# Second FFN block of a transformer layer: where the late tokens' pieces are loaded from, and on which queue

## The chip, the cores and the metric

One Trainium2 chip, one of its cores. The metric is device time in microseconds (us) of the whole kernel, one launch; a lower number is better. Five engines run side by side, each through its own instruction queue: TensorE (PE in the profile; PEld are its weight loads), VectorE (DVE), ScalarE (ACT), GpSimd (POOL) and SyncE (SP). SP, ACT and POOL can also issue DMA transfers. "SPq" and "POOLq" in a row mean the issue of a DMA on that queue.

## The reference

One layer for 128 context tokens and 1024 latent tokens of width 1024, all in float32:

```python
x <- LN(alpha*x + 0.5 * gate1 * SwiGLU_1(mod1(x)))     # first FFN block
x <- LN(alpha*x + gate2 * Mixer(mod2(x)))              # attention, pooling, gates
x <- LN(alpha*x + 0.5 * gate3 * SwiGLU_2(mod3(x)))     # second FFN block

def _modulate(x, shift, scale):
    return x * (1.0 + scale) + shift

def _swiglu(h, w1, w2):                                # w1: 1024 x 5632, w2: 2816 x 1024
    a, b = jnp.split(h @ w1, 2, axis=-1)
    return (jax.nn.silu(a) * b) @ w2
```

Only the second FFN block (`SwiGLU_2`) and the way its input comes out of the mixer matter here.

## The kernel before

Every float32 product is three matmuls: `split` (L107 on ACT, L108 on DVE) makes a high and a low part of each operand, and `mm3` (L130 to L132) adds high-high, high-low and low-high. The FFN products are arranged as Strassen-like sums: seven products of half blocks in place of eight, so both operands also have to be added and subtracted before they are split.

The latent tokens form two halves of 512: half n = 0 is tokens 0 to 511 of the latent rows, half n = 1 the late tokens. For each half and each of the 8 blocks of 128 channels (`kc`) there is one *piece*, a 128 x 512 tile. `piece_dram(n, kc)` makes one: it loads a token-major block from `x2_d[1 + n]` (the mixer's result, in DRAM), transposes it on PE in four 128 x 128 steps (L135) into a PSUM bank, and modulates it on ACT (L402) into its final place. One such load is 256 KB in 512 runs of 512 bytes.

`x2_d` is written by `norm_tile` as the mixer's last token tiles are normalized (L350, a DMA on POOL's queue, tile names `x<-ry`). The last group of three token tiles holds the end of the late half, so half n = 1 is complete only when the last of those stores has landed. These last normalizations run inside `lead_first`, beside the products `A11` of the first four feature blocks.

Then `lead` runs with `begun` true. In program order it does: `second` (product `A12`) for p = 0 to 3; `first_sum` (weights minus weights, L711) for four p, two loads each; four pieces of half 0 into `self.first`; then for k = 0 to 3 `sum_operands` (L457), which takes pieces (1, k) and (1, k+4), adds them and splits the sum into `S1[k]` (tile `b`), each followed by the units of product `S1` for p = 0 and 1; product `S1` for p = 2; the other four pieces of half 0; product `S1` for p = 3; `next_operand` (`S2`, L462); and then the products `S2`, `S4`, `S3`, `A22` with their weights (L738, L752, L756) and `last_operands` (L468, L471).

Two sets of places matter. `raw_tile` is a ring of 5 places of 4 KB per partition through which nearly all raw loads go, weights and pieces alike, all issued on SP's queue in order; a load waits there until the place it takes is free. The tag `b2` has 12 places of 4 KB per partition: in this block eight of them first hold the pieces of half 0 (tile `xp`), and later all are used for the left operands `S3`, `S4` and `A22`. The pieces of half 1 end in tile `pc`. Instructions are put into each engine's queue at build time by a scheduler which takes, in program order, those that it thinks are ready; so the order within a queue can differ from the order in the code, and is fixed before the kernel runs.

Of the kernel before, what the change touches and what calls it, by code (L numbers as in the profile page):

```python
# [25 lines left out]
F32 = mybir.dt.float32  # L26
# [6 lines left out]
P = 128  # L33
# [21 lines left out]
class Layer:  # L55
# [362 lines left out]
        return m  # L418

    def piece_dram(self, n, kc):  # L420
        r = self.raw(self.x2_d[1 + n][:, :, kc * P : (kc + 1) * P], 512)
        b = self.bank()
        for t in range(4):
            self.transpose(b[:, t * P : (t + 1) * P], r[:, t * P : (t + 1) * P])
        m = self.piece_place(n, kc)
        self.modulated(m, b, 2, LAT, kc)
        return m
# [1256 lines left out]
```

## Time and profile before

| | |
|---|---|
| median of 3 runs | 2496.45 us (2493.36 to 2497.18) |
| the profiled execution | 2495.49 us, its span 2493.7 us |
| granted TensorE clock, mean | 0.995 |
| PE busy | 2452.3 us (98% of the span) |
| DVE busy | 1830.6 us (73%) |
| ACT busy | 1214.5 us (49%) |
| POOL busy | 463.4 us (19%) |
| DMA, SP's queue | 373.79 MB, 44.7% of 16 engines' span |
| DMA, POOL's queue | 86.32 MB, 9.3% of 16 engines' span |

PE is busy nearly all of the span, so the time is read from where PE is idle and from what ends each of its idle stretches. "Released by" means the event that came last before the waiting instruction began. Share figures are averages over the span; a change in one stage is read from that stage alone.

### The profile page before, as it was taken

What the parts mean: (1) busy time and instruction counts of PE and PEld (TensorE: products, weight loads), DVE (VectorE), ACT (ScalarE), POOL (GpSimd) and SP (SyncE); (2) the same over time, 40 slices, a digit from 0 to 9 for tenths busy, and PEclk for the clock granted to TensorE, in tenths of its full rate; (3) what the DMA queues carried; (4) which work ended last, traced back from release to release, by engine and by line L of the source; (5) the groups of instructions that cost most, each with busy time, mean ns of one, the idle gap of its engine ahead of it and who ended that gap; (6) DMA issues with size and microseconds to landing.
All of it is one profiled execution on the core that took longest, in us unless ns stands there. A gap on an engine that the chain in (4) does not pass through costs nothing.

```text
span 2493.7 us, 34226 instructions
## 1 busy us (share of the span) xinstructions
PE 2452.3 (98%) x12297; PEld 2115.0 (85%) x12297; DVE 1830.6 (73%) x2817; ACT 1214.5 (49%) x2094; POOL 463.4 (19%) x691
## 2 busy tenths in 40 slices
PE   8999999999999999999999999999899999999998
PEld 4788888888889989889999999998688888887887
DVE  6877778877678556566888886876877666676877
ACT  5544444444445343434778773435744344444442
POOL 0000011110022212232567640110000001111002
PEclk9999999999999999999999999999999999999999
DMA  7455566778686555534100035665754445558773
GB/s 292 144 167 188 182 224 230 244 259 326 213 276 218 184 180 189 188 136 163 42 1 2 1 110 187 237 215 185 223 173 164 150 173 195 205 197 320 269 267 121
DMA packets 167554, 463.75 MB, mean 186 GB/s; under 512 B 18900, under 2 KB 37636, under 8 KB 167384
## 3 DMA queue, kind: packets, MB, share of 16 engines
q1 hardware_dynamic: 140952, 373.79, 44.7%
q0 software_dynamic: 23696, 86.32, 9.3%
q8 instruction: 97, 1.59, 0.3%
q10 hardware_dynamic: 2736, 1.44, 0.2%
q14 instruction: 73, 0.60, 0.1%
HBM read 390.42 MB, written 71.07 MB: 185 GB/s over the span
## 4 chain that ended last, share of the span: by engine, by line
PE 84%; DVE 6%; issue 4%; DMA 3%; ACT 2%; POOL 1%; SPq 0%; DVEq 0%; POOLq 0%; ACTq 0%
PE w L130 24%; PE w L131 24%; PE w L132 24%; PE w L1060 8%; PE w L135 3%; DVE op L108 1%; DVE x L108 1%; DMA raw<-w 1%; DVE mx L1389 1%; PE w L224 0%; DMA yc<-fc 0%; ACT pr L1397 0%; DMA raw<-w1c 0%; DVE so L108 0%; DMA raw<-x 0%
## 5 line engine op out<-in xcount | busy, mean ns | idle before, releaser
L107 ACT ACTIVATE op<-raw 128x1024 fp32r<-128x1024 f32 (+1 forms) x505 | 483.9, 969 | 517.4 <-PE w L131 263.4
L108 DVE TENSOR_TENSOR op<-raw,op 128x1024 fp32r<-128x1024 f32 (+1 forms) x505 | 558.9, 1116 | 233.1 <-ACT op L107 201.1
L130 PE MATMUL w<-b,op 128*128 128x512 f32 x880 | 343.9, 393 | 7.1 <-ACT b L107 2.9
L131 PE MATMUL w<-b,op 128*128 128x512 f32 x880 | 344.6, 392 | 0.0
L132 PE MATMUL w<-b,op 128*128 128x512 f32 x880 | 339.7, 391 | 0.3 <-DVE op L108 0.3
L130 PE MATMUL w<-x,op 128*128 128x384 f32 x768 | 260.0, 339 | 0.0
L131 PE MATMUL w<-x,op 128*128 128x384 f32 x768 | 258.8, 337 | 0.0
L132 PE MATMUL w<-x,op 128*128 128x384 f32 x768 | 257.7, 337 | 0.0
L131 PE MATMUL w<-op,so 128*128 128x512 f32 (+1 forms) x627 | 242.4, 387 | 2.0 <-DVE op L108 2.0
L132 PE MATMUL w<-op,so 128*128 128x512 f32 (+1 forms) x627 | 241.9, 387 | 0.0
L130 PE MATMUL w<-op,so 128*128 128x512 f32 (+1 forms) x627 | 232.7, 386 | 1.0 <-ACT op L107 0.9
L130 PEld LDWEIGHTS w<-b,op 128*128 128x128 f32 x880 | 165.6, 188 | 42.9 <-ACT b L107 3.4
L562 POOL DMA_DIRECT2D h<-tmp x80 | 43.4, 543 | 851.6 <-DVE tmp L626 426.1
L132 PEld LDWEIGHTS w<-b,op 128*128 128x128 f32 x880 | 165.8, 188 | 35.8 <-DVE op L108 0.8
L131 PEld LDWEIGHTS w<-b,op 128*128 128x128 f32 x880 | 165.8, 188 | 34.8 <-DVE b L108 0.7
L1402 POOL TENSOR_TENSOR pr<-pr,sm 128x384 f32<-128x384 f32 x192 | 156.1, 842 | 95.1 <-DVE sm L1400 71.8
L190 DVE SCALAR_TENSOR_TENSOR junk<-raw,sil 128x1024 bf16<-128x1024 f32 x112 | 135.9, 1224 | 26.0 <-DMA raw<-w_mod 25.6
L107 ACT ACTIVATE so<-sr 128x1024 fp32r<-128x1024 f32 (+1 forms) x84 | 82.7, 986 | 136.1 <-PE w L131 82.7
L131 PEld LDWEIGHTS w<-x,op 128*128 128x128 f32 x768 | 144.1, 188 | 0.3
L130 PEld LDWEIGHTS w<-x,op 128*128 128x128 f32 x768 | 144.1, 188 | 0.4
L132 PEld LDWEIGHTS w<-x,op 128*128 128x128 f32 x768 | 143.9, 188 | 0.0
L131 PEld LDWEIGHTS w<-op,so 128*128 128x128 f32 x627 | 118.2, 189 | 26.8 <-DVE op L108 3.2
(323 smaller groups left out, 5136.6 us busy)
## 6 DMA issues: line engine op xcount, KB each, us to landing
raw<-w SPq DMA_DIRECT2D x240, 256.0 KB, 5.3
raw<-w SPq DMA_DIRECT2D x116, 512.0 KB, 3.9
raw<-w1c SPq DMA_DIRECT2D x80, 512.0 KB, 4.0
sr<-h SPq DMA_DIRECT2D x70, 512.0 KB, 5.7
raw<-w_mod SPq DMA_DIRECT2D x56, 512.0 KB, 4.3
raw<-w_gate SPq DMA_DIRECT2D x48, 512.0 KB, 3.7
h<-tmp POOLq DMA_DIRECT2D x80, 256.0 KB, 3.6
h<-pc POOLq DMA_DIRECT2D x52, 256.0 KB, 4.6
```

The costliest lines, as they stand in the source:

```text
L107: self.nc.scalar.activation(hi, src, AF.Copy)
L108: self.nc.vector.tensor_tensor(lo, src, hi.bitcast(F32), ALU.subtract)
L130: mm(out, lhsT=lh, rhs=rh, start=start, stop=False)
L131: mm(out, lhsT=lh, rhs=rl, start=False, stop=False)
L132: mm(out, lhsT=ll, rhs=rh, start=False, stop=stop)
L135: self.nc.tensor.transpose(out, src, self.ident)
L190: nc.vector.scalar_tensor_tensor(junk, w, 1.0, self.sil[cond], ALU.mult, ALU.mult, accum_out=self.mod[:, cond, b : b + 1],)
L562: self.nc.gpsimd.dma_start(h_d[f // 2][:, 2 * kh + n, f % 2, :], h)
L1060: self.nc.tensor.matmul(acc[h][j], lhsT=lhs[:, part, js], rhs=w[wi][:, h * 512 : (h + 1) * 512], start=f, stop=l)
L1389: nc.vector.tensor_reduce(mx[:, c : c + 1], b[:, :GT], AX.X, ALU.max)
L1402: nc.gpsimd.tensor_tensor(pr[:, c, :], pr[:, c, :], sm[:, 3:4].broadcast_to([P, GT]), ALU.mult)
```

## The change

In `piece_dram`, the load of a piece of half n = 1 no longer takes a place of the `raw` ring and no longer goes through SP's queue. It takes a place of tag `b2` (tile name `xr`, half of a 4 KB place used) and is issued on POOL's queue. Pieces of half 0 are loaded as before. Eight loads are concerned; the transposes, the modulation and everything behind them are the same code.

```diff
     def piece_dram(self, n, kc):
-        r = self.raw(self.x2_d[1 + n][:, :, kc * P : (kc + 1) * P], 512)
+        src = self.x2_d[1 + n][:, :, kc * P : (kc + 1) * P]
+        if n == 0:
+            r = self.raw(src, 512)
+        else:
+            r = self.pools["b2"].tile([P, 512], F32, tag="b2", name=self.name("xr"), bufs=12)
+            self.nc.gpsimd.dma_start(r.rearrange("p (a b) -> p a b", a=4), src)
         b = self.bank()
```

## Rows read from the trace of the kernel before

**Rows 1.** Windows: busy us (instructions) per engine, granted clock, DMA share, GB/s

```profile
1756.00:1800.00 44.00, 36.66 (x180) 27.64 (x179) 32.39 (x47) 29.18 (x44) 1.57 (x3) 1.00 0.72 217
1800.00:2100.00 300.00, 300.00 (x1317) 245.27 (x1316) 213.92 (x286) 130.31 (x178) 21.75 (x39) 1.00 0.49 169
```

**Rows 2.** Waits of PE, 1690 to 1900 us: total us, times, longest

```profile
PE w L135 <- DMA raw<-x: 3.0, 5, 1.5
PE w L130 <- ACT b L107: 2.9, 2, 2.3
PE w L135 <- ACT xp L402: 0.8, 2, 0.6
PE w L132 <- DVE op L108: 0.3, 1, 0.3
```

**Rows 3.** Timeline of PE: start, us, instruction, [idle before it, and its releaser]

```profile
1770.90 0.66 PE L135 MATMUL w<-ident,raw 128*128 128x128 f32 x4 [1.49 <-DMA raw<-x]
...
1773.60 0.63 PE L135 MATMUL w<-ident,raw 128*128 128x128 f32 x4 [0.24 <-ACT xp L402]
...
1778.73 0.73 PE L130 MATMUL w<-b,op 128*128 128x512 f32 x2 [2.25 <-ACT b L107]
```

**Rows 4.** Timeline of SP's queue: start, us from first to last issue, count

```profile
1760.14 5.71 SPq L111 DMA_DIRECT2D raw<-w  x8
1766.18 18.52 SPq L111 DMA_DIRECT2D raw<-x  x16
```

**Rows 5.** Waits of SP's queue, 1730 to 1800 us

```profile
SPq L111 <- PE w L135: 15.8, 12, 3.1
```

**Rows 6.** Chain that ended last, 1740 to 1830 us: start, us, what

```profile
1772.21 3.50 DMA raw<-x
...
1776.51 0.79 ACT pc L402
1777.32 0.70 DVE pc L457
1778.05 0.64 ACT b L107
...
1785.54 3.19 DMA raw<-w
```

**Rows 7.** Windows of 5 and 20 us, same columns as rows 1

```profile
1765.00:1770.00 5.00, 4.18 (x17) 2.75 (x15) 4.79 (x7) 1.79 (x3) 0.00 (x0) 1.00 0.97 302
1770.00:1790.00 20.00, 14.42 (x82) 10.86 (x82) 10.58 (x17) 14.61 (x24) 0.00 (x0) 1.00 0.75 212
```

**Rows 8.** Timeline of POOL: last store of x2, and its next instruction

```profile
1758.67 0.60 POOL L350 DMA_DIRECT2D x<-ry  x1 [1.62 <-DVE ry L349]
1821.66 0.55 POOL L562 DMA_DIRECT2D h<-tmp  x1 [62.39 <-DVE tmp L748]
```

**Rows 9.** DMA issues, 1756 to 1800 us: KB each, median us to landing

```profile
raw<-x SPq DMA_DIRECT2D x16, 256.0 KB, 3.6
x<-ry POOLq DMA_DIRECT2D x1, 512.0 KB, 3.1
```

**Rows 10.** DMA issues, whole span: the kernel's existing piece-like loads on POOL

```profile
xr<-x POOLq DMA_DIRECT2D x4, 384.0 KB, 8.4
```

**Rows 11.** Groups by line on POOL: busy us, mean ns | idle before

```profile
L562 POOL DMA_DIRECT2D h<-tmp x80 | 43.4, 543 | 851.6 <-DVE tmp L626 426.1 <-DVE tmp L617 242.8 <-DVE tmp L748 170.5
...
L574 POOL DMA_DIRECT2D h<-raw x22 | 15.8, 718 | 44.7 <-DVE raw L573 44.7
...
L274 POOL DMA_DIRECT2D xr<-x x4 | 3.1, 788 | 9.4 <-PE w L135 9.1 <-issue 0.3
```

**Rows 12.** DMA queues, 746 to 752 us: packets, MB, share of 16 engines

```profile
q0 software_dynamic: 198, 0.72, 34.5%
```

**Rows 13.** DMA queues, 1773 to 1775 us, same columns

```profile
q1 hardware_dynamic: 1101, 0.55, 95.6%
```

**Rows 14.** Windows: the stretch behind the sums, columns of rows 1

```profile
1788.00:1817.00 29.00, 28.06 (x126) 21.91 (x125) 28.24 (x46) 20.03 (x36) 0.00 (x0) 1.00 0.49 155
```

## The prediction

> **What bounds the kernel now.** I read the windows first, to see where PE is idle. From 1756 to 1800 us it is busy 36.66 of 44.00 us, so 7.34 us are idle; in the next 300 us it is busy all 300 [rows 1]. The change touches eight loads that are used inside those 44 us and nothing else, so 7.34 us (0.29% of the time) is nearly all that it can win, and any microsecond by which PE gets through this stretch sooner is kept, because PE is the bound behind it. Next come PE's waits: 3.0 us for pieces to land before their transposes, 2.9 us for the first sums S1 to be split, 0.8 us for a PSUM bank that ACT empties, 0.3 us for an operand that DVE splits [rows 2]. The timeline says when: PE's A12 products end at about 1769.4 us, the first piece's transposes start at 1770.90, and the first matmul on S1 is at 1778.73 [rows 3]. In the 9.3 us between, PE has only six groups of transposes of about 0.65 us, of which those rows show the first and the fourth.
>
> The chain shows what makes S1 late. A piece of half 1 is issued at 1772.21, lands 3.50 us later, is transposed (0.65), modulated (0.79), added to its partner (0.70) and split (0.64), with small gaps: 1778.73 [rows 6]. So from landing to PE it takes about 3.0 us, and what comes before is the load. Why is it issued only at 1772? SP's queue issues sixteen pieces from 1766.18 on, after eight weight loads [rows 4], and they wait 15.8 us in twelve waits for transposes to free a place in the ring of five [rows 5]. The four pieces of half 0 go first. The data of half 1 has been in DRAM far longer: its last store was issued at 1758.67 [rows 8] and landed 3.1 us later [rows 9], at 1761.8.
>
> **The change part by part.** *SP's queue loses eight issues* of about 0.5 us. SP isn't limited by that but by places, so those 4 us are worth nothing by themselves. What counts is the eight turns of the ring: behind the last piece stands the weight load of 1785.54, which lands 3.2 us later and from which S2's operand is made [rows 6]. It can now move up, by at most the length of eight of the sixteen turns, half of 18.5 us [rows 4]. Its cover is good, since S2 comes after all S1 products.
>
> *POOL's queue gains eight issues.* The trace has no POOL load of 512 runs. The nearest rows are 128 runs at 543 ns, 256 at 718 ns and 384 at 788 ns [rows 11]; continuing this I take 0.87 us (bounds 0.79 and 1.05), so 8 x 0.87 = 7.0 us, from 1761.8 (POOL waits for the store's landing) to about 1769. Nothing is queued behind them: POOL's next instruction is at 1821.66, after 62.39 us of idleness [rows 8]. That idleness is the cover, and nobody is kept waiting by POOL. It also sits idle itself while it waits for the landing.
>
> *Landing of the new loads.* On SP a piece takes 3.6 us [rows 9]; the kernel's only similar loads on POOL, 1.5 times as large, took 8.4 us under a full DMA load [rows 10]. For 256 KB I take 5 us for the first two, with 3.6 and 8.4 as bounds: pieces (1,0) and (1,4) would be there by 1767.6 (1766.3 to 1771.1) instead of 1775.7, and the others about every 0.9 to 1.6 us behind.
>
> *Places.* Four pieces of half 0 and eight new loads are exactly the 12 places of b2. The other four pieces of half 0 take places that transposes have freed by then, and S3, S4 and A22 need theirs only when the last operands are made, after S2. The memory below b2 belonged to the mixer's last stage, whose final reader is that same store of 1758.67. I cost the places at nothing; if that fails, a piece of half 0 waits for one transpose, 0.65 us.
>
> *Contention.* This is the real cost. DMA is already 0.97 busy at 302 GB/s from 1765 to 1770, and 0.75 on the mean of the next 20 us [rows 7]. Eight weight loads, eight new loads and four pieces of half 0 are 20 x 0.262 = 5.2 MB; at 302 GB/s that takes 17.4 us from about 1760.5, so the last of them lands near 1778. Of the early ones, some must land later than before. What suffers are the weight differences for p = 2 and 3 (used only after four S1 sums, so some 8 us of cover) and the first pieces of half 0, which in program order come first but aren't needed before S2. So it matters little if they are late, provided that PE's queue does not have their transposes ahead of half 1's. I expect the scheduler, which picks what it thinks ready, to see half 1 ready first and order it so.
>
> The Trainium skill speaks against this change: the page "DMA: Bandwidth & Descriptors", section "Issuing engines are not separate DMA queues", says that transfers issued from different engines share the same 16 DMA engines, so a second queue saves only issue time. By that rule the sum would be zero. The trace agrees where the share is 0.97, but a quarter of the 20 us behind it is unused, 5 us in all, and by these holes the gain could be up to as much [rows 7].
>
> *Sum.* With half 1 first, after 1769.4 PE does two groups of transposes (1.3 us), and then the 2.1 us of modulation, sum and split pass, in which it can do none to four more groups of transposes: 1.0 to 3.4 us idle where there are about 6 now. Of the later waits (0.6 for the second S1, 0.6 for a bank, 0.3 for an operand [rows 2]) 0 to 1.5 us stay. So 1.0 to 4.9 us of 7.34 stay and 2.4 to 6.3 us are won. I take the middle, 4.3 us, since DVE comes next: it is busy 28.24 of 29 us from 1788 [rows 14], with 9.4 us of idleness in the 20 us from 1770 [rows 7], which can be used only as fast as the pieces come. Against its own time the profiled execution would go from 2495.49 to 2491.2 us; that execution stands 0.96 us below the median of the three runs, so against the median it is 2492.2, which I put down as 2492.
>
> **Rivals.**
>
> *A. The DMA engines or DVE bind, and most of the gain is lost.* If the order on PE stays as it is and the pieces of half 0 land 1 to 2 us later, S1 begins after the fourth of them: transposes of it and of two pieces, then 2.1 us. Before, the fourth was transposed at 1773.60 [rows 3]; from there the same steps give 1773.6 + 0.65 + 1.3 + 2.1 = 1777.7, a gain of 1.1 us, less the delay, plus up to 1.5 us of later waits. That is 0 to 2.6 us won: 2493.9 to 2496.5. For it speaks the busy DMA; against it the holes in the windows.
>
> *B. Slower: POOL's transfers starve SP's.* POOL's loads of 1 KB runs went out in 198 packets for 0.72 MB, 3.6 KB each [rows 12]; SP's pieces in 1101 for 0.55 MB, 0.5 KB each [rows 13]. If the engines share by packet, POOL's 2.1 MB go first almost whole, and SP's pieces of half 0 are set back by up to 2.1 MB at 302 GB/s, 7 us: the fourth is transposed not at 1773.6 but at up to 1780.6. If PE's queue has these transposes ahead of half 1's, S1 begins at 1780.6 + 4.1 = 1784.7, 6 us late; with 1.5 us of later waits gone that is 4.5 us slower, near 2501, and at 5 us of delay 2.4 us slower, near 2499. It decides from the point where the fourth piece is more than 2.6 us late (1.1 + 1.5). Against it: the first three weight pairs are on their way before POOL can start, and ready pieces of half 1 give PE other work if they come first.
>
> The same page of the Trainium skill, section "Queues, rings and completion order", states that each engine goes round its queues packet by packet; no run here shows by itself how it shares between packets of such different size.
>
> *C. The change does not do what it says.* The build orders the new loads late on POOL, or the new order of all instructions behind the lead costs something where PE has no idle time now [rows 1]. Then 2495 to 2499.
>
> **How the numbers follow.** Forecast 0.50 (2490.1 to 2494.1 by the bounds of the sum), A 0.27, B 0.13, C 0.10. About 0.2% of this time, 5 us, is what a measurement can tell from no change. More than 5 us needs the upper third of the forecast's range or a start that is better by all bounds (PE never idle: 7.3 us, 2489.1); with the scatter of a median of three that is 0.5 of the forecast's chance and a little of A: 0.28. Slower by over 5 us: half of B and a little of C, 0.08. Between them 0.64. The range runs from 2489.5 to 2499.5: it leaves out the case of no idle time at all and the worse half of B.
>
> **What would show it.** Right: on POOL eight issues from about 1762, none over 1.1 us; the first S1 matmul at 1771 to 1775 instead of 1778.73; PE's wait for pieces and S1 down from 5.9 to under 3.5 us; the load for S2's difference issued before 1783; and PE without idle time behind 1800. Wrong: transposes of half 0 ahead of half 1 on PE with waits of over 2 us (B), DVE as the releaser of PE's waits near 1790 (A), or new waits of PE behind 1800 (C).

## The result: slower, and where the time went

The median went from 2495.96 us (6 runs, 2493.36 to 2497.18) to **2510.47 us** (6 runs, 2509.29 to 2512.46): a ratio of 1.0061 [1.0050, 1.0072], 14.5 us slower. The forecast of 2492 was wrong, in its sign too, and the time lies outside its range. The two profiled executions stand 17.0 us apart (2512.46 and 2495.49); that of after is 2.0 us above its median.

Nearly all of it lies in the stretch that the change touches and in the 40 us behind it. The windows of after, which answer to [rows 1] (columns as there):

```profile
1756.00:1800.00 44.00, 25.81 (x108) 20.06 (x107) 22.32 (x31) 20.00 (x29) 6.22 (x9) 0.73 0.62 185
...
1817.00:1840.00 23.00, 19.70 (x81) 15.55 (x80) 16.43 (x26) 13.81 (x23) 0.56 (x1) 0.93 0.22 73
```

PE is idle for 18.19 of the 44 us, where 7.34 were idle before, and for 3.30 us more behind 1817, where PE was idle for none before. That is 14.15 us of new idleness. The rest is longer busy time. The profiled executions of different kernels reach this stretch up to 7.3 us apart, so from here on times are counted from PE's first matmul of A11, at 1735.17 us before and 1733.07 after. From there to the end the same 3314 PE instructions take 740.99 us before and 745.49 us after, 4.5 us more (windows of before, then of after):

```profile
1735.17:2600.00 864.83, 740.99 (x3314) 606.65 (x3312) 553.12 (x708) 338.61 (x453) 77.84 (x115) 0.99 0.52 181
1733.07:2600.00 866.93, 745.49 (x3314) 611.03 (x3312) 553.41 (x708) 339.29 (x453) 84.03 (x123) 0.98 0.52 180
```

The granted clock has fallen to 0.73 and 0.93 in the two stretches above, where it was 1.00, and that goes with it. So counted, the rest of the span is 19.1 us longer (777.6 against 758.5): 14.6 us of idleness and 4.5 us of busy time. The 17.0 us are less by the 2.1 us by which this execution of after reached A11 sooner.

PE's waits of after, 1690 to 1900 us, answer to [rows 2]:

```profile
PE w L130 <- ACT b L107: 8.4, 1, 8.4
PE w L135 <- DMA raw<-x: 4.8, 1, 4.8
PE w L131 <- DVE op L108: 3.9, 1, 3.9
PE w L131 <- DVE b L108: 2.3, 1, 2.3
PE w L130 <- ACT xp L402: 1.0, 1, 1.0
```

The timeline of PE in after, which answers to [rows 3]:

```profile
1769.84 0.80 PE L131 MATMUL w<-op,xm 128*128 128x512 f32 x1 [3.95 <-DVE op L108]
...
1776.76 3.76 PE L135 MATMUL w<-ident,raw 128*128 128x128 f32 x16 [4.84 <-DMA raw<-x]
1780.31 1.64 PE L135 MATMUL w<-ident,xr 128*128 128x128 f32 x8
1790.39 1.22 PE L130 MATMUL w<-b,op 128*128 128x512 f32 x2 [8.43 <-ACT b L107]
...
1824.81 0.50 PE L131 MATMUL w<-b,op 128*128 128x512 f32 x1 [2.29 <-DVE b L108]
```

Three waits stand ahead of the first S1 matmul: for the last operand of A12, for the first piece of half 0 (all four of its transpose groups still come first, in one run of 16 transposes), and, behind the first two `xr` groups, 8.43 us for S1 itself. Counted from A11's first matmul, the first S1 matmul stood at 43.6 us before and stands at 57.3 after: **13.8 us later**. The part up to the first `xr` transposes is 7.4 us of it (47.24 against 39.84 for the same fifth group of transposes before, the one at 1775.01); the 8.43 us wait, where 2.25 us stood before [rows 3], is 6.2 of the other 6.4.

**The first part: who got the DMA engines.** The timeline of POOL in after:

```profile
1759.24 5.24 POOL L426 DMA_DIRECT2D xr<-x  x7 [3.02 <-DMA x<-ry]
1766.72 0.75 POOL L426 DMA_DIRECT2D xr<-x  x1 [2.23 <-DMA xr<-x]
1838.44 0.56 POOL L567 DMA_DIRECT2D h<-tmp  x1 [70.98 <-DVE tmp L753]
```

SP's queue in after (it answers to [rows 4]):

```profile
1757.52 6.45 SPq L111 DMA_DIRECT2D raw<-w  x8
1764.01 16.43 SPq L111 DMA_DIRECT2D raw<-x  x8
```

The DMA issues from 1756 to 1768 us, of before and then of after (KB each, median us to landing):

```profile
raw<-w SPq DMA_DIRECT2D x8, 256.0 KB, 4.5
```

```profile
raw<-w SPq DMA_DIRECT2D x8, 256.0 KB, 10.3
xr<-x POOLq DMA_DIRECT2D x8, 256.0 KB, 9.3
```

Seven of POOL's eight loads go out one behind the other from 1759.24, as soon as the last store has landed, right into SP's eight weight loads and the first pieces of half 0; the eighth waits 2.23 us until an earlier `xr` has landed, and why it does is not shown. They themselves take 9.3 us, but the weight loads now take 10.3 us where they took 4.5, and the first piece of half 0 takes 12.7 (chain below), where a piece took 3.6 [rows 9]. How the 16 engines are shared shows in the view of the DMA queues (packets, MB, share), first from 1764 to 1768 us of after:

```profile
q0 software_dynamic: 209, 0.68, 52.5%
q1 hardware_dynamic: 329, 0.60, 46.8%
```

and then from 1768 to 1772 us:

```profile
q0 software_dynamic: 251, 0.82, 65.1%
q1 hardware_dynamic: 264, 0.48, 39.5%
```

POOL's packets are some 3.3 KB, SP's some 1.8 KB here. From 1768 on the two queues send nearly as many packets each, so nearly two thirds of the bytes are POOL's; in the four microseconds before SP sends more packets, and POOL has about half of the bytes. The Trainium skill, page "DMA: Bandwidth & Descriptors", section "Queues, rings and completion order", states that each engine goes round its queues by packets. The counts from 1768 to 1772 agree with that, those before it leave it open.

**The second part: the order on DVE.** The timeline of DVE in after:

```profile
1767.96 0.69 DVE L716 TENSOR_TENSOR ts<-raw 128x512 f32<-128x512 f32 x1 [4.33 <-DMA raw<-w]
1768.57 1.22 DVE L108 TENSOR_TENSOR op<-raw,op 128x1024 fp32r<-128x1024 f32 x1
...
1784.90 0.69 DVE L743 TENSOR_TENSOR ts<-raw,ts 128x512 f32<-128x512 f32 x1 [4.97 <-DMA raw<-w]
...
1788.38 0.69 DVE L743 TENSOR_TENSOR ts<-raw,ts 128x512 f32<-128x512 f32 x1 [1.39 <-DMA raw<-w]
1788.98 0.68 DVE L462 TENSOR_TENSOR pc<-pc,pc 128x512 f32<-128x512 f32 x1
```

The same view of before, the fourth sum of S1 and the first difference of S2:

```profile
1786.36 0.69 DVE L457 TENSOR_TENSOR pc<-pc,pc 128x512 f32<-128x512 f32 x1
...
1788.76 0.69 DVE L738 TENSOR_TENSOR ts<-raw,ts 128x512 f32<-128x512 f32 x1 [1.10 <-DMA raw<-w]
```

The last row of after is S1's first sum (L457 of before). Its two pieces were transposed by 1782, but ahead of it in DVE's queue stand two weight differences of *S2* (L743, L738 of before), whose loads SP issues only from 1780.55 on. Before, DVE's first L738 came behind the first four of these sums. The scheduler fixes this order when the kernel is built; with the loads of half 1 elsewhere it put S2's differences first. The trace shows the order that came out, not the scheduler's reason. The first two rows of after belong to the first part: the split of A12's last operand stands behind a difference that waits 4.33 us for its late pair of weights. It stood behind one before too, which waited 0.18 us; here only the landing is new. The chain of after ties the parts together, 1764 to 1791 us (between these two rows stand the 16 transposes of half 0):

```profile
1764.01 12.70 DMA raw<-x
...
1780.55 4.33 DMA raw<-w
```

### The profile page after: what moved, and what is told of

It reads as the page before. It is cut to its first block, busy times and chain, and to the rows that moved or that the text cites. A ratio compares the mean times of both kernels' runs of the same rounds, so it can differ in the third digit from the quotient of the medians.

```text
span 2510.7 us, 34228 instructions
## 1 busy us (share of the span) xinstructions
PE 2455.7 (98%) x12297; PEld 2120.2 (84%) x12297; DVE 1829.8 (73%) x2817; ACT 1216.2 (48%) x2094; POOL 467.8 (19%) x699
## 4 chain that ended last, share of the span: by engine, by line
PE 84%; DVE 6%; issue 4%; DMA 3%; ACT 2%; POOL 1%; SPq 0%; DVEq 0%; POOLq 0%; ACTq 0%
PE w L130 24%; PE w L131 24%; PE w L132 24%; PE w L1065 8%; PE w L135 3%; DMA raw<-w 1%; DVE op L108 1%; DMA raw<-w_mod 1%; DVE x L108 1%; DVE mx L1394 1%; DMA raw<-x 1%; ACT pr L1402 0%; PE w L224 0%; ACT pc L402 0%; DVE pl L1327 0%
## 5 line engine op out<-in xcount | busy, mean ns | idle before, releaser
L567 POOL DMA_DIRECT2D h<-tmp x80 | 43.6, 545 | 853.9 <-DVE tmp L631 438.3
```

Of the source, the lines that this page charges most:

```text
L567: self.nc.gpsimd.dma_start(h_d[f // 2][:, 2 * kh + n, f % 2, :], h)
```

## The experiments

Theories: **contention** (POOL's loads start early, all at once, and take the engines from transfers that are due sooner), **order** (S2's weights ahead of S1's sum on DVE and ACT), and the rival that the **places** or POOL's queue cost something by themselves. All kernels were timed against the kernel before on the same chip. "us slower" below is the difference of the medians; the ratio need not be the quotient of the medians.

| kernel | first S1 matmul behind A11's first, us | against before | median, us | before, us | ratio |
|---|---|---|---|---|---|
| before | 43.6 | | | | |
| after | 57.3 | +13.8 | 2510.47 | 2495.96 | 1.0061 [1.0050, 1.0072] |
| e3_dummy | 52.1 | +8.5 | 2503.44 | 2494.28 | 1.0038 [1.0023, 1.0053] |
| e4_s1first | 50.3 | +6.7 | 2501.51 | 2494.28 | 1.0029 [1.0016, 1.0042] |
| e8_half_dose | 46.1 | +2.5 | 2498.43 | 2494.56 | 1.0016 [1.0007, 1.0026] |
| e2_ring_pool | 43.6 | 0.0 | 2496.33 | 2494.56 | 1.0005 [0.9995, 1.0014] |
| e5_sp_s1first | 49.1 | +5.5 | 2501.52 | 2494.28 | 1.0025 [1.0016, 1.0035] |
| e1_sp | 48.9 | +5.4 | 2504.45 | 2494.28 | 1.0043 [1.0028, 1.0058] |
| e6_swap | 39.1 | -4.5 | 2494.35 | 2494.56 | 1.0001 [0.9991, 1.0010] |
| e7_pool_swap | 39.9 | -3.6 | 2495.93 | 2494.56 | 1.0002 [0.9992, 1.0011] |
| e10_swap_fill | 40.0 | -3.5 | 2495.18 | 2494.28 | 1.0005 [0.9997, 1.0014] |
| e12_pool_swap_fill | 42.4 | -1.2 | 2500.29 | 2494.28 | 1.0022 [1.0012, 1.0031] |

The profiled executions, one of each kernel, tell the same when their time is counted from A11's first matmul to the end of the span. Against before it is 19.1 us longer in after, 9.5 in e3_dummy, 6.5 in e4_s1first, 3.3 in e8_half_dose, 1.6 in e2_ring_pool, 6.6 in e5_sp_s1first, 9.5 in e1_sp, -0.3 in e6_swap, 0.8 in e7_pool_swap and 6.8 in e12_pool_swap_fill. Only after and e10_swap_fill (3.8) stand 3 to 5 us above what their medians say.

**e3_dummy: contention alone.** The kernel before, with its own loads and its own order, plus the eight POOL loads of the change into places of `b2` that nothing reads:

```diff
+        if n == 1:
+            d = self.pools["b2"].tile([P, 512], F32, tag="b2", name=self.name("xd"), bufs=12)
+            self.nc.gpsimd.dma_start(d.rearrange("p (a b) -> p a b", a=4), src)
         r = self.raw(src, 512)
```

> The kernel before, with eight extra loads on POOL's queue into places of b2 (the same 256 KB blocks of the late half, issued at the same place, read by nobody); the order of the lead's instructions on PE, DVE, ACT and SP is that of before. It leaves nothing out and adds 2.1 MB of traffic. Theory (POOL's transfers delay SP's): the weight pairs and the first pieces of half 0 land 9 to 13 us after issue instead of 4 to 5, the first S1 matmul is 7 to 10 us later, and the time is 2502 to 2506 us. Rival (only the order of DVE's and ACT's queues cost time, the transfers did no harm): within 2 us of before, 2494 to 2498. Rival (both small, low clock of PE did it): within 4 us of before.

Measured: 9.2 us slower, with the first S1 matmul 8.5 us later, both as the theory expected. DMA issues from 1757 to 1766 us of e3_dummy:

```profile
raw<-w SPq DMA_DIRECT2D x8, 256.0 KB, 10.3
xd<-x POOLq DMA_DIRECT2D x7, 256.0 KB, 9.0
```

PE of e3_dummy:

```profile
1776.90 3.76 PE L135 MATMUL w<-ident,raw 128*128 128x128 f32 x16 [5.73 <-DMA raw<-x]
...
1785.60 1.22 PE L130 MATMUL w<-b,op 128*128 128x512 f32 x2 [2.26 <-ACT b L107]
```

The weight loads take 10.3 us (median) and the first pieces make PE wait 5.73 us, as in after; the wait for S1 is the 2.26 us of before. So transfers that nobody waits for cost 8.5 us ahead of S1. (2.1 MB are moved twice here, so this is somewhat more than the change's own contention.)

**e4_s1first: the order undone.** The changed kernel, with S2's weight differences and their splits held behind the last split of S1:

```diff
-            sub(T[p], r, T[p])
-            prod(Y[p], "S2", self.wide(T[p], 512), False)
+            if begun:
+                with self.tc.issue_after(s1_lo), self.tc.issue_after(s1_hi):
+                    sub(T[p], r, T[p])
+                    w = self.wide(T[p], 512)
...
+            prod(Y[p], "S2", w, False)
```

> The changed kernel, with the subtraction and split of S2's weights held behind the last split of S1 on DVE and on ACT, which is the order that the kernel before has; the eight loads stay on POOL's queue in b2. Theory (two causes, contention about 8 us and order about 6 us): 2503 to 2506 us, landings as in the changed kernel (9 to 13 us), first S1 matmul 5 to 6 us sooner than in the changed kernel. Rival (order alone): back to 2494 to 2498. Rival (contention alone): stays at 2509 to 2512.

Measured: 7.2 us slower than before, where the change is 14.5 slower; that is 1.5 us under the range of the theory of two causes, and outside both rivals. S1 comes 7.1 us sooner than in after, where 5 to 6 were expected, and what is left of its delay is 6.7 us. PE of e4_s1first:

```profile
1775.72 3.79 PE L135 MATMUL w<-ident,raw 128*128 128x128 f32 x16 [5.02 <-DMA raw<-x]
...
1783.47 0.73 PE L130 MATMUL w<-b,op 128*128 128x512 f32 x2 [2.25 <-ACT b L107]
```

The wait for S1 is back at 2.25 us; the wait for the pieces stays. So by the medians the order is half of the loss, and contention the other.

**e8_half_dose: half the transfers.** As e4_s1first, but only pieces (1,0) to (1,3) go to POOL; (1,4) to (1,7) go through SP and the ring:

```diff
-        if n == 0:
+        if n == 0 or kc >= 4:
             r = self.raw(src, 512)
```

> The changed kernel with S2's weights held behind S1 (as in e4_s1first), and only four of the eight pieces, (1,0) to (1,3), on POOL's queue in b2; (1,4) to (1,7) in the ring on SP's queue. Theory (the delay goes with the bytes that run ahead): the weight pairs land 7 to 9 us after issue, and the time is about midway between before (2494.3) and e4_s1first (2501.5): 2496 to 2500 us. Rival (a fixed cost of having loads on POOL at all): 2501 to 2503. The kernel computes everything.

Measured: 3.9 us slower, against 7.2 with all eight, within the range of the theory. S1 is 2.5 us late, against 6.7. The four loads land in 6.8 us (median), where the eight of e4_s1first take 8.1, and the eight weight loads in 8.3, where they take 11.0 there. The intervals of the two times overlap, those landings and the place of S1 are far apart. So the delay goes with the bytes that start early, outside the ring; that it is not simply the bytes on POOL's queue shows the next kernel.

**e2_ring_pool: POOL's queue kept, the places undone.** The eight loads stay on POOL but take places of the ring:

```diff
-            r = self.pools["b2"].tile([P, 512], F32, tag="b2", name=self.name("xr"), bufs=12)
+            r = self.raw_tile()[:, :512]
```

> The changed kernel with only the places undone: the eight loads are issued on POOL's queue, but into the ring of five raw places. A load can then start only when a place is free, so it can't run ahead of the weight pairs and of half 0. Theory (the loss comes from eight transfers started at once ahead of data that is needed sooner, not from the queue as such): weight pairs and first pieces land in 4 to 6 us, first S1 matmul 19 to 22 us after the last store of x2 is issued (before: 20.1), time 2493 to 2498 us. Rival (POOL's queue is slow by itself, whoever it competes with): 2500 us or more.

Measured: no difference from before (ratio 1.0005, the interval holds 1), and S1 to the tenth where it was. POOL's first loads in e2_ring_pool:

```profile
1770.66 1.53 POOL L426 DMA_DIRECT2D raw<-x  x2 [13.69 <-DMA raw<-x]
```

Its DMA issues, first SP's from 1756 to 1768 us, then POOL's from 1750 to 1800 us:

```profile
raw<-w SPq DMA_DIRECT2D x8, 256.0 KB, 4.4
```

```profile
raw<-x POOLq DMA_DIRECT2D x8, 256.0 KB, 4.2
```

On the ring, POOL waits for a place as SP did and starts only at 1770.66, when the weight loads and half 0 are through; the weight loads take 4.4 us (median), as before. So it isn't POOL's queue that costs. It is the places outside the ring: the wait for a place, which the change removes, was what kept the loads in the order of need.

**e5_sp_s1first and e1_sp: the queue undone, the places kept.** The loads go to `b2` through SP's queue; e5_sp_s1first has the hold of e4_s1first as well.

```diff
-            self.nc.gpsimd.dma_start(r.rearrange("p (a b) -> p a b", a=4), src)
+            self.load(r.rearrange("p (a b) -> p a b", a=4), src)
```

> The changed kernel with the eight loads in their places of b2 but on SP's queue, and the same hold on S2's weights. No load of the lead is on POOL's queue. Theory (POOL's queue is the cause): landings of the weight pairs and first pieces back at 4 to 5 us, time 2494 to 2501 us (the late half now stands behind all of half 0 in SP's order, which can cost up to 4 us). Rival (the places in b2 are the cause, for example by waiting for memory of the mixer's last stage): 2503 us or more.

> The changed kernel with only the queue undone: the eight loads in b2, on SP's queue; the scheduler's order puts S2's first weight difference ahead of S1's first sum on DVE, as in the changed kernel. Theory: without POOL's transfers the weights land in time and most of the loss goes: 2496 to 2503 us, and 1 to 5 us more than the same with S1 first. Rival (order alone is the cause): 2506 us or more.

Measured: 7.2 and 10.2 us slower; e5_sp_s1first lies half a microsecond and e1_sp 1.5 us above what was expected of them, both below their rivals. This isn't POOL against SP any more, yet the loss stays, by another road. SP's queue in e5_sp_s1first:

```profile
1766.00 8.84 SPq L111 DMA_DIRECT2D raw<-x  x8
1775.33 0.33 SPq L111 DMA_DIRECT2D raw<-w  x1
1775.77 6.64 SPq L111 DMA_DIRECT2D xr<-x  x8
```

PE of the same kernel:

```profile
1780.82 1.97 PE L135 MATMUL w<-ident,xr 128*128 128x128 f32 x8 [5.52 <-DMA xr<-x]
```

All eight pieces of half 0 and one of S2's weight loads now stand in SP's queue ahead of the first piece of half 1, where four stood before, and PE waits 5.52 us for it. So with the ring's places the loads lose their order on SP as well. The two kernels have their first S1 at the same place; e1_sp's other 2.9 us go with a wait of 3.20 us behind 1818 (PE for the split of a later `b`), which e5_sp_s1first has not. The intervals of the two times overlap; counted from A11 the profiled executions differ by the same 2.9 us. That the wait is gone with the hold is what the pair shows; how, was not followed further.

**e7_pool_swap and e6_swap: half 1 first.** The prediction rested on PE taking half 1's transposes first. Here the code says so: the first four pieces of half 0 are made behind the four sums S1, in the changed kernel (e7_pool_swap) and in the kernel before (e6_swap).

```diff
-            self.first = [piece(0, k) for k in R]
             X = [self.bank() for _ in range(2)]
...
                     self.up_unit(X[p], "S1", W[p], k, k == 0, k == 3)
+            self.first = [piece(0, k) for k in R]
             for p in (2, 3):
```

> The changed kernel with the same move: half 1 on POOL's queue in b2, and half 0's first pieces made behind S1[0..3]. Theory (the harm is in what the eight transfers overtake; with this order they overtake pieces that S1 does not need): landings of SP's loads stay long (8 to 12 us), but the first S1 matmul comes 16 to 19 us after the last store of x2, and the time is 2489 to 2497 us. Rival (contention harms whatever the order): 2500 us or more.

> The kernel before with one move: the first four pieces of half 0 are made behind the sums S1[0..3] instead of ahead of them; queues and places as before. Theory (PE waits for half 1 to land, and four pieces that are not needed yet stand ahead of it): first S1 matmul 3 to 4 us sooner, 16 to 17 us after the last store of x2, time 2489 to 2493 us against 2494.3. Rival (DVE or the DMA engines bind the stretch as a whole): 2493.5 to 2496.

Measured: neither differs from before. For e7_pool_swap that is within the theory's range; for e6_swap the theory's gain failed, and the time is the rival's. In e7_pool_swap all 14.5 us of the change's loss are gone, though POOL's loads still land late. Its DMA issues from 1750 to 1768 us:

```profile
raw<-w SPq DMA_DIRECT2D x8, 256.0 KB, 8.6
xr<-x POOLq DMA_DIRECT2D x8, 256.0 KB, 8.6
```

PE of e7_pool_swap:

```profile
1761.75 0.65 PE L135 MATMUL w<-ident,xr 128*128 128x128 f32 x4 [1.67 <-DMA xr<-x]
...
1768.59 1.22 PE L130 MATMUL w<-b,op 128*128 128x512 f32 x2 [3.42 <-ACT b L107]
```

Half 1's transposes come first now, so half 0's late pieces are no longer at the head of PE's queue, and on DVE all four sums of S1 come ahead of S2's differences, so this kernel undoes both parts of the loss. What is left of the contention is the weights: S1's first sum on DVE (1767.19) stands behind a difference that waits 2.54 us for its pair. S1 comes 3.6 us sooner than before, in e6_swap, without the change, 4.5, and in both no time is won. Windows of e6_swap:

```profile
1766.00:1771.00 5.00, 1.49 (x9) 0.84 (x8) 3.90 (x7) 3.63 (x6) 0.00 (x0) 0.94 0.89 257
1771.00:1776.00 5.00, 4.87 (x17) 4.09 (x18) 1.39 (x2) 2.00 (x4) 0.00 (x0) 0.50 0.40 114
```

PE is idle for 3.5 of 5 us, and in the next 5 us the granted clock is 0.50 (1.2 GHz): 4.87 busy us do only 17 matmuls and transposes. At a clock of 1.00 that work would be about half as long, so by this estimate up to 2.4 us of the 4.5 go there; from A11's first matmul to the end PE's busy time is only 1.0 us above that of before. The profile has one more wait of 1.5 us, for ACT, at 1789.5. Where the whole 4.5 us went is not settled.

**e10_swap_fill and e12_pool_swap_fill: the clock kept up.** e6_swap and e7_pool_swap with 10 and 12 matmuls without use, into a bank that S1 then starts anew, behind the first pair's transposes:

```diff
+                if k == 0:
+                    a = self.A["A12"]
+                    with self.tc.issue_after(self.last_t):
+                        for j in range(10):
+                            nc.tensor.matmul(X[0], lhsT=a[j % 4][0][:, :P], rhs=a[j % 4][0], start=True, stop=True, skip_group_check=True)
```

> e6_swap with ten further 128x512 matmuls on PE (about 2.3 us) between the transposes of the first pair of half 1 and the first matmul on S1, into a bank that the product S1 then starts afresh; they add nothing to the result. In e6_swap PE waited there, the granted clock fell to 0.50 for some 6 us behind the wait, and the 3 us by which S1 came sooner were lost again. Theory (the low clock took the gain): clock 1.00 over the whole stretch, first S1 matmul still about 17 us after the last store of x2, time 2490 to 2493 us, 0.05 to 0.15% below before. Rival (DVE, ACT or the DMA engines bind the stretch behind S1): 2493.5 to 2496 us, with new waits of PE in place of the slow matmuls.

> e7_pool_swap (half 1 on POOL's queue in b2, half 0's first pieces behind S1) with twelve such filler matmuls at the same place. Theory (in e7_pool_swap too it was the low clock that kept the gain away): clock 1.00 over the stretch, time 2490 to 2494 us. Rival (POOL's transfers delay half 0 and S2's weights so far that S2 becomes the wait): 2494.5 to 2498 us.

Measured: 0.9 us above before (the interval holds 1) and 6.0 us slower. Both theories failed in the time: e10_swap_fill has that of its rival, e12_pool_swap_fill lies above both ranges. In e10_swap_fill the clock did as expected. The window of e10_swap_fill:

```profile
1771.00:1776.00 5.00, 4.61 (x28) 3.46 (x26) 2.11 (x4) 2.61 (x5) 0.00 (x0) 1.00 0.63 183
```

PE of e10_swap_fill, its longest later wait:

```profile
1805.16 0.79 PE L130 MATMUL w<-b,op 128*128 128x512 f32 x1 [3.79 <-ACT xp L402]
```

DVE of e12_pool_swap_fill:

```profile
1773.25 0.69 DVE L716 TENSOR_TENSOR ts<-raw 128x512 f32<-128x512 f32 x1 [4.59 <-DMA raw<-w]
```

PE of e12_pool_swap_fill:

```profile
1810.06 0.58 PE L130 MATMUL w<-b,op 128*128 128x512 f32 x1 [4.02 <-ACT xp L402]
```

In e10_swap_fill the clock is 1.00 in that window, with 28 matmuls and transposes instead of 17. But each edit makes the build order the queues anew, and in both PE now waits some 4 us later on for a bank that ACT empties. In e12_pool_swap_fill DVE has a difference for a late weight pair ahead of S1's sum, the pattern of after in small. So that the clock slows e6_swap's stretch is shown; that holding it up wins the time back is not. No kernel that was run is faster than the one before.

## Why the prediction was wrong, step by step

- **"I expect the scheduler, which picks what it thinks ready, to see half 1 ready first and order it so."** This is the step that failed first. PE's queue kept the four transpose groups of half 0 ahead, and the first S1 matmul came 13.8 us later. With half 1 first in the code (e7_pool_swap) S1 does come 3.6 us sooner, just short of the 3.7 to 7.7 us that the signs of being right asked for (1771 to 1775 instead of 1778.73). So the gain at S1 was argued for an order that the change doesn't make.
- **"... any microsecond by which PE gets through this stretch sooner is kept".** This failed too, and it would have sunk the forecast with the right order: S1 is 3.6 us sooner in e7_pool_swap and 4.5 in e6_swap, and neither time differs from before.
- **The sum's terms.** "1.0 to 3.4 us idle" does not follow from its steps: 2.1 us with none to four groups of 0.65 us in them leave 2.1 to 0 us idle. And by [rows 2] the idleness up to S1 is 5.5 us (3.0 for pieces, 2.3 for S1, 0.2 for a bank), not about 6.
- **Contention, judged by the last landing and not by the first ones.** The total was right (POOL's last load is issued at 1766.72 and none takes over 10.9 us, so all are there by 1777.6; 1778 was worked out). But I looked at when the last load lands and let "some" of the early ones land later, with some 8 us of cover. The early ones are the ones that PE, DVE and ACT have at the head of their queues: weight loads of 10.3 us, a first piece of 12.7. Rival B is this mechanism. It had the trigger (the fourth piece more than 2.6 us late) and half 0's pieces up to 7 us late; the transposes behind them came 7.4 us late. S1 was to be 6 us late, and is 6.7 in e4_s1first. Its price of 4.5 us was under the 7.2 of e4_s1first, since it took 1.5 us of later waits for gone, where 2.5 us stand in e4_s1first, and had no term for the clock. What it held against itself was misread: at the pace of [rows 4], three weight loads and not three pairs are issued in the 1.7 us before POOL starts.
- **"Its cover is good, since S2 comes after all S1 products."** This holds on PE and fails on DVE and ACT. I asked what stands behind POOL's new issues, and not what the build would do to the other queues: S2's differences moved ahead of S1's sum. This is 6.2 us on the timeline and 7.3 us by e4_s1first, and no rival of mine had it. Rival C named a new order behind the lead, at no more than 4 us, and not inside it.
- **Places "at nothing".** In after no load of the eight is released by a reader of its place, which fits. But the 15.8 us for which SP's queue waited for places [rows 5] were counted as a delay to be saved; e2_ring_pool and e5_sp_s1first show that they also kept the loads in the order of need.
- **The clock** was taken as 1.00 throughout [rows 1, 7]. It went to 0.50 behind the new idle stretches, and PE's busy time behind A11's start grew by 4.5 us.
- **Landing of the new loads:** 5 us taken, 3.6 to 8.4 as bounds; measured 9.3, above the bounds. The row with the full DMA load [rows 10] was the nearer one.
- **Right:** POOL's issues (0.75 to 0.78 us each, 0.87 taken, the bounds missed by 0.04 at most), their start behind the store's landing (3.0 us, 3.1 taken), POOL's cover (70.98 us idle behind them), and DMA as the thing that limits.
- **The page that spoke against the change.** The Trainium skill, page "DMA: Bandwidth & Descriptors", section "Issuing engines are not separate DMA queues", states that starting transfers on several engines saves issue time only. From this I had worked out a sum of zero. Even zero was too good: e3_dummy shows that loads on a second queue, started early, cost 9.2 us by what they take from the first. I had set its rule aside for the holes in the DMA windows [rows 7]; these holes lie behind 1770, while the new loads were all issued by 1768 and the engines moved 323 GB/s from 1764 to 1772.

Of the marks set for right and wrong, those of B came (transposes of half 0 ahead, waits of 4.84 us) and C's (new waits behind 1800, of 1.0 and 2.3 us). For S1's wait the releaser was ACT behind DVE behind a load, one step further back than rival A looked.

## What to carry to other kernels

A wait for a place in a ring is also what keeps loads in the order of need: before taking loads out of it, list what is in flight when they then start, and which engine has that at the head of its queue. Where a scheduler orders the queues at build, an edit of a load can move work on engines that the edit doesn't name; ask for each in-order queue what could now stand ahead of the critical step, and if the answer matters, write the order down. And a gain that rests on an order must be given that order: with it (e7_pool_swap) the same loads did no harm, though no good either.

## What the runs showed of the hardware that I had not expected

- Of two DMA queues with work, the one with the larger packets got more of the bytes: 0.82 MB to 0.48 at 251 packets to 264 (after, 1768 to 1772 us). Over all of 1764 to 1772 us it was 1.50 MB to 1.08.
- The eight weight loads of 256 KB that take 4.5 us before and 4.4 in e2_ring_pool took 10.3 in after and in e3_dummy, by eight loads on another queue.
- The granted clock of TensorE fell to its lower level (0.50, 1.2 GHz) behind a stretch in which PE was idle 3.5 of 5 us (e6_swap), and in after in these windows, columns of rows 1:

```profile
1785.00:1790.00 5.00, 0.00 (x0) 0.00 (x0) 2.76 (x5) 2.80 (x5) 0.00 (x0) 0.50 0.17 52
1790.00:1795.00 5.00, 4.61 (x15) 3.82 (x16) 3.10 (x5) 2.30 (x4) 0.00 (x0) 0.50 0.32 105
```

After the 8.43 us wait PE works for the next 5 us at the lower level, so this wait cost more than its own length. A wait alone doesn't tell whether the clock falls: behind 2.25 us for S1 it stayed at 1.00 before, behind 2.26 us in e2_ring_pool it was 0.70 from 1780 to 1785 us.
